# One DRAM replication of 5 MB issued as eight transfers, in a one-core hybrid attention and mLSTM layer

## The chip, the core and the metric

The kernel runs on one core of one Trainium2 chip. Times are device microseconds (us) of that core. The kernel before takes 886.04 us in the median of three runs (885.03 to 887.89). One further execution was recorded with the profiler; all durations below come from it.

## The reference

A decoder layer on 512 tokens of 1024 channels. The input is RMS-normalised and projected once; two branches read the projection, each is gated, projected back, and the two are merged, projected, added to the input and normalised. What matters here is where the position bias comes from.

```
proj = xn @ w_in[layer]
q_a, k_a, v_a, z_a, x_m, z_m, o_m, gates = jnp.split(proj, SPLIT_POINTS, axis=-1)
y_a = dilated_attention(to_heads(q_a), to_heads(k_a), to_heads(v_a), rel_bias)   # 16 heads of 64
y_a = (y_a * jax.nn.silu(z_a)) @ w_pa[layer]
y_m = mlstm_branch(x_m, z_m, o_m, ...) @ w_pb[layer]                             # 4 heads of 512
merged = g_a * y_a + g_m * y_m
h = h + (merged @ w_out[layer]).astype(h.dtype)
# inside the attention, for each head:
bias = rel_bias.astype(jnp.float32)[t5_bucket(jnp.clip(delta, 0, band) * dilation)]
logits = jnp.where(valid, logits + bias, -jnp.inf)
```

The bias depends on the distance between query and key alone, so for one head it is one row of numbers, read at a shifted place for each query.

## The kernel before, in words

**Stages.** Products in f32 precision are made of three fast products each: every operand is split into a high part (`whi`, `xh`, made by ScalarE, ACT) and a low part (`wlo`, `xl`, made by VectorE, DVE), and TensorE (PE) multiplies high by high, high by low and low by high. Weights come in 512 KB chunks (`raw`, 128 rows of 4096 bytes) from DRAM. In order of time PE makes the projection `xm` and the mLSTM scores `S`, then for each of the four mLSTM heads: the output gate `om`, the values `v` (from a copy `xmr` of the projected rows that was stored in DRAM), the numerators `num`, the gate `zm`, the transposes `hT`, and the projection `ym`. Then comes `va`, the values of eight attention heads, and the eight pairs of attention heads (`qa`, `ka`, `za`, `sa`, `pT`, `pv`), the merge gates `gate`, and the projections `ya` and `out`.

**The bias rows.** After the first mLSTM head the function `rel_rows` makes the 16 bias rows of 640 numbers, stores them in DRAM as `fd`, and copies `fd` inside DRAM into `fr`, which holds each row 128 times: 16 x 128 x 640 numbers, 5120 KB, in one transfer. Each attention head later loads its tile `tb` from `fr` with a row step of 639, which gives every partition the row shifted by one.

**What sets the order.** Nothing runs while the kernel is written down: every call is recorded, and a list planner (`Recorder.issue`) replays the recording with estimated durations and writes out one instruction order for each engine. All loads but the last store go through one queue, that of SyncE (SP). A load is placed when its buffer is free in the plan; of the waiting ones the planner looks at about forty in the order of the recording, so a transfer that is recorded late is placed late although nothing holds it. At run time each engine, and SP too, takes its list strictly in order.

**Names and lines.** All instructions carry L333, the line where the recorded calls are made, so the text goes by tiles. `weights` (L423) loads and splits one chunk; `pair_weights` (L573) does it for two chunks that are combined (`s`); `block_v` (L746) loads four `xmr` and makes `v`; `values` (L1019) makes `va` out of four chunks; `rel_rows` is L995.

Of the kernel before, what the change touches and what calls it, by code (L numbers as in the profile page):

```python
# [17 lines left out]
P = 128  # L18
# [6 lines left out]
HEADS_A = 16  # L25
# [312 lines left out]
def hybrid_layer(ctx, tc, a, out):  # L338
    nc = tc.nc
    R = Recorder(nc, a["win"].tensor)  # L340
    V, A, PE, G, SP = (R.engine(e) for e in ("vector", "scalar", "tensor", "gpsimd", "sync"))
# [11 lines left out]
    def slot(name, dt=F32):  # L353
        return tile_of(upool, [P, 516], dt, name, "u", NSLOT)

    def mm_bank(name):
        return tile_of(psum, [P, 512], F32, name, "mm", 2, True)

    def sc_bank(name):
        return tile_of(psum, [P, 512], F32, name, "x", 6, True)  # L360
# [3 lines left out]
    def wide(name, dt=F32):  # L364
        return tile_of(upool, [P, 1280], dt, name, "w1280", NWIDE)

    def wide_t(name, dt=F32R):
        return tile_of(upool, [P, 1408], dt, name, "w1408", NWT)

    def small(name, n):  # L370
        return tile_of(spool, [P, 8], F32, name, "small", NSMALL)[:, :n]

    def const(name, shape, dt=F32):
        return R.buf(lambda: cpool.tile(shape, dt, name=name), shape, dt)

    def raw_chunk(name, p=P):
        return tile_of(wpool, [P, 1024], F32, name, "raw", NRAW)[:p]

    def dram(name, shape):
        return R.buf(lambda: dpool.tile(shape, F32, name=name), shape, F32, dram=True)  # L380
# [42 lines left out]
    def weights(src):  # L423
        R.ahead = AHEAD
        hl = halves(fetch(src))
        R.ahead = 0
        return hl
# [22 lines left out]
    def proj_k(ps, hl, x, k):  # L450
        c = slice(k * P, (k + 1) * P)
        mm3(ps, hl[0][:, c], hl[1][:, c], *x[k], k == 0, k == NK - 1)
# [192 lines left out]
    def proj_t(chunk, name, x=None):  # L645
        hl = weights(a["win"][chunk])
        ps = mm_bank(name)
        for k in range(NK):
            proj_k(ps, hl, x or list(zip(xh, xl)), k)
        return ps  # L650
# [235 lines left out]
    def silu2(ps, name):  # L886
        z = slot(name)[:, :T]
        A.activation(z, ps, AF.Tanh, scale=0.5)
        V.scalar_tensor_tensor(z, z, 1.0, ps, op0=OP.add, op1=OP.mult)
        return z  # L890
# [104 lines left out]
    def rel_rows():  # L995
        onehot = raw_chunk("onehot", 64)[:, :640]
        SP.dma_start(onehot, a["onehot"])
        relb = const("relb", [32, HEADS_A], F32)
        SP.dma_start(relb, a["rel_bias"])
        ohr, rel2 = wide("ohr", F32R)[:64, :640], const("rel2", [64, HEADS_A], F32R)  # L1000
        A.activation(ohr, onehot, AF.Copy)
        A.activation(rel2[:32], relb, AF.Copy)
        V.tensor_sub(rel2[32:], relb, rel2[:32].bitcast(F32))
        lnm = raw_chunk("lnm", 16)[:, :640]
        SP.dma_start(lnm, a["lnmask"])
        frow = raw_chunk("frow", 16)[:, :640]
        for c0 in (0, 320):
            ps = sc_bank("frow")[:16, :320]
            PE.matmul(ps, rel2, ohr[:, c0:c0 + 320], start=True, stop=True)
            V.tensor_add(frow[:, c0:c0 + 320], ps, lnm[:, c0:c0 + 320])  # L1010
        fd = dram("fd", [16, 640])
        SP.dma_start(fd, frow)
        fr = dram("fr", [16, P, 640])
        SP.dma_start(fr, fd[:, None, :].to_broadcast([16, P, 640]))
        return fr

    vals = []

    def values(p):  # L1019
        vv = []  # L1020
        for ps in proj_n(CV + p, "va"):
            for c in range(2):
                v = slot("va", F32R)[:, :512].rearrange("p (h w c) -> p h w c", h=4, w=2)
                src = ps[:, 256 * c:256 * c + 256].rearrange("p (h c) -> p h c", h=4)
                R.ahead = EMPTY
                A.activation(v[:, :, 0, :], src, AF.Copy, scale=0.5)
                V.scalar_tensor_tensor(v[:, :, 1, :], src, 0.5, v[:, :, 0, :].bitcast(F32),
                                       op0=OP.mult, op1=OP.subtract)
                R.ahead = 0
                vv.append(v)  # L1030
        return vv

    wt_of[0] = head_weights(0)
    for h in range(HEADS_M):
        head(h)
        if h == 0:
            fr = rel_rows()


    yaf = []  # L1040
    for p in range(HEADS_A // 2):
        if p % 4 == 0 and p:
            vals.append(values(p))
        vv = vals[-1]
        qps = proj_t(CQ + p, "qa")
        qh = [slot("qh", F32R)[:, :T] for _ in range(2)]
        ql = [slot("ql", F32R)[:, :T] for _ in range(2)]
        for w in range(2):
            o, o2 = 64 * w, 64 - 64 * w
            src = qps[o:o + 64]  # L1050
            A.activation(qh[w][o:o + 64], src, AF.Copy, scale=0.125)
            V.scalar_tensor_tensor(ql[w][o:o + 64], src, 0.125, qh[w][o:o + 64].bitcast(F32),
                                   op0=OP.mult, op1=OP.subtract)
            A.activation(qh[w][o2:o2 + 64], qh[w][o:o + 64].bitcast(F32), AF.Copy)
            A.activation(ql[w][o2:o2 + 64], ql[w][o:o + 64].bitcast(F32), AF.Copy)
        kps = proj_t(CK + p, "ka")
        kk = [slot("kk", F32R)[:, :T] for _ in range(2)]
        for w in range(2):
            src = kps[64 * w:64 * w + 64]
            o, o2 = 64 * w, 64 - 64 * w  # L1060
            A.activation(kk[w][o:o + 64], src, AF.Copy)
            V.tensor_sub(kk[w][o2:o2 + 64], src, kk[w][o:o + 64].bitcast(F32))
        z = silu2(proj_t(CZA + p, "za"), "za")
        ya = slot("ya")[:, :T]
        tmp = slot("yt")[:, :T]
        for w in range(2):
            hd = 2 * p + w
            tb = slot("tb")[:, :512]
            SP.dma_start(tb, fr[hd].then(lambda r: bass.AP(tensor=r.tensor, offset=r.offset + 127,
                                                           ap=[[639, P], [1, 512]])))  # L1070
            pt = wide("p")
            pr = []
            for i in range(NT):
                n = P * (i + 1)
                N = max(n, 256)
                ps = sc_bank("sa")
                qq = slice(i * P, (i + 1) * P)
                PE.matmul(ps[:, :N], qh[w][:, qq], kk[w][:, :N], start=True, stop=False)
                PE.matmul(ps[:, :N], ql[w][:, qq], kk[w][:, :N], start=False, stop=True)
                s = pt[:, P * (i * (i + 1) // 2):][:, :n]  # L1080
                mx, sm = small("mx", 1), small("sm", 1)
                V.tensor_tensor_reduce(s, ps[:, :n], tb[:, 512 - n:], op0=OP.add, op1=OP.min, scale=-1.0,
                                       scalar=3.0e38, accum_out=mx)
                A.activation(s, s, AF.Exp, scale=-1.0, bias=mx, accum_out=sm)
                V.reciprocal(sm, sm)
                V.tensor_scalar(s, s, sm, None, op0=OP.mult)
                pr.append(s)
            po = pv_bank("pv")
            pth, ptl = wide_t("pTh"), wide_t("pTl")
            off = (0, 512, 896, 1152)  # L1090
            for j in range(NT):
                t0 = j * P
                q0 = min(t0, T - 256)
                ps = sc_bank("pT")
                for i in range(j, NT):
                    PE.transpose(ps[:, i * P:(i + 1) * P], pr[i][:, t0:t0 + P], ident)
                th, tl = pth[:, off[j]:off[j] + T - q0], ptl[:, off[j]:off[j] + T - q0]
                if q0 < t0:
                    G.memset(th[:, :t0 - q0].bitcast(F32), 0.0)
                    G.memset(tl[:, :t0 - q0].bitcast(F32), 0.0)  # L1100
                A.activation(th[:, t0 - q0:], ps[:, t0:], AF.Copy)
                V.tensor_sub(tl[:, t0 - q0:], ps[:, t0:], th[:, t0 - q0:].bitcast(F32))
                lv = vv[2 * j + p % 4 // 2][:, 2 * (p % 2) + w].rearrange("p w c -> p (w c)")
                PE.matmul(po[:, q0:], lv, th, start=j == 0, stop=False)
                PE.matmul(po[:, q0:], lv, tl, start=False, stop=j == NT - 1)
            o, o2 = 64 * w, 64 - 64 * w
            A.activation(tmp[o:o + 64], po[o2:o2 + 64], AF.Copy)
            V.tensor_add(ya[o:o + 64], po[o:o + 64], tmp[o:o + 64])
        V.tensor_mul(ya, ya, z)
        yaf.append(ya)  # L1110
# [178 lines left out]
```

## Time and profile before

| what | us |
|---|---|
| median of three runs | 886.04 |
| the profiled execution's own time | 883.73 |
| its span, from the first to the last instruction | 881.8 |
| PE busy | 863.8 (98% of the span) |
| DVE busy | 661.8 (75%) |
| ACT busy | 471.2 (53%) |
| mean share of full clock granted to PE | 0.996 |
| data moved by DMA | 110.00 MB, 125 GB/s in the mean |

The profiled execution took 1.9 us more than its span, for what lies ahead of the first and behind the last instruction. Busy time of PE is modelled, so 98% says that PE has hardly any idle time, not that it is at its peak. The DMA line of the page shows the load on the core's 16 DMA engines: it is heavy in the first 60 us and again around 265 to 290 us, and light elsewhere.

### The profile page before, as it was taken

To read this page: it belongs to the slowest core of one execution; us is meant where nothing else is said; L and a number is where in the kernel's file an instruction comes from. 1 tells how busy PE (TensorE), PEld (TensorE's weight loads), DVE (VectorE), ACT (ScalarE), POOL (GpSimd) and SP (SyncE) were. 2 spreads that over 40 slices of the span, in tenths; PEclk is the share of its full clock that TensorE was granted. 3 is DMA by queue.
4 is the path that set the end of the run, shared out by engine and by line. 5 is a ranking of instruction groups with operands and counts; after the bars stand their busy time and mean duration, and the time that the engine had idled before them with its cause. 6 is when DMAs were issued, how large, how long until landed. Compare 5 with 4: busy or idle time off the path is not lost.

```text
span 881.8 us, 13364 instructions
## 1 busy us (share of the span) xinstructions
PE 863.8 (98%) x4916; PEld 741.7 (84%) x4916; DVE 661.8 (75%) x1361; ACT 471.2 (53%) x879; POOL 10.9 (1%) x70
## 2 busy tenths in 40 slices
PE   7999999999998999999999999999999999999997
PEld 6778877798888889988988888888888899998886
DVE  4899889799557867967865487874778899888533
ACT  7668876655323522551333477654667665674222
POOL 0000000000000000000000000000000000000000
PEclk9999999999999999999999999999999999999999
DMA  9834443234339422511424322212222123356021
GB/s 317 318 132 161 162 166 116 89 123 150 102 121 335 149 72 96 199 61 52 159 81 144 120 82 87 97 60 96 83 77 80 61 73 119 119 170 214 25 72 48
DMA packets 39962, 110.00 MB, mean 125 GB/s; under 512 B 4436, under 2 KB 6228, under 8 KB 39896
## 3 DMA queue, kind: packets, MB, share of 16 engines
q1 hardware_dynamic: 39752, 108.87, 36.0%
q8 instruction: 39, 0.64, 0.3%
q10 hardware_dynamic: 144, 0.26, 0.1%
q14 instruction: 27, 0.22, 0.1%
HBM read 95.97 MB, written 18.39 MB: 130 GB/s over the span
## 4 chain that ended last, share of the span: by engine, by line
PE 89%; DMA 6%; DVE 2%; ACT 1%; SPq 1%; issue 0%; POOL 0%; ACTq 0%
PE ym L333 10%; PE om L333 10%; PE gate L333 9%; PE zm L333 7%; PE xm L333 7%; PE out L333 5%; PE va L333 5%; PE ya L333 5%; PE qa L333 5%; PE za L333 5%; PE ka L333 4%; DMA raw<-in_win_dram 4%; PE S L333 3%; PE num L333 2%; PE sa L333 2%; PE pv L333 2%
## 5 line engine op out<-in xcount | busy, mean ns | idle before, releaser
L333 DVE TENSOR_TENSOR wlo<-raw,whi 128x1024 fp32r<-128x1024 f32 (+1 forms) x126 | 146.9, 1170 | 81.4 <-ACT whi L333 81.0
L333 ACT ACTIVATE whi<-raw 128x1024 fp32r<-128x1024 f32 (+1 forms) x126 | 127.8, 1017 | 145.6 <-PE ym L333 44.8
L333 ACT ACTIVATE whi<-s 128x512 fp32r<-128x512 f32 (+1 forms) x32 | 26.9, 841 | 51.1 <-PE ym L333 11.9
L333 PE MATMUL om<-whi,xh 128*128 128x512 f32 x128 | 51.1, 399 | 0.0
L333 PE MATMUL om<-whi,xl 128*128 128x512 f32 x128 | 50.7, 396 | 0.0
L333 PE MATMUL ym<-yh,whi 128*128 128x512 f32 x128 | 50.7, 396 | 0.0
L333 PE MATMUL om<-wlo,xh 128*128 128x512 f32 x128 | 50.6, 395 | 0.0
L333 PE MATMUL ym<-yl,whi 128*128 128x512 f32 x128 | 50.5, 395 | 0.0
L333 PE MATMUL ym<-yh,wlo 128*128 128x512 f32 x128 | 50.4, 394 | 0.0
L333 ACT ACTIVATE p<-p,mx 128x128 f32<-128x128 f32 (+1 forms) x64 | 35.6, 558 | 14.5 <-DVE mx L333 14.2
L333 DVE CUSTOM_DVE_ANT_0 p<-sa,tb 128x128 f32<-128x128 f32 (+1 forms) x64 | 28.8, 484 | 14.4 <-PE sa L333 14.4
L333 PE MATMUL zm<-th,whi 128*128 128x256 f32 x128 | 36.9, 288 | 0.0
L333 PE MATMUL zm<-tl,whi 128*128 128x256 f32 x128 | 36.5, 285 | 0.0
L333 PE MATMUL zm<-th,wlo 128*128 128x256 f32 x128 | 36.5, 286 | 0.0
L333 PE MATMUL gate<-th,wlo 128*128 128x256 f32 x128 | 36.3, 284 | 0.0
L333 PE MATMUL gate<-tl,whi 128*128 128x256 f32 x128 | 36.1, 282 | 0.0
L333 PE MATMUL gate<-th,whi 128*128 128x256 f32 x128 | 35.9, 282 | 0.0
L333 DVE SCALAR_TENSOR_TENSOR conv<-xm,half,conv 128x512 f32<-128x512 f32 x48 | 35.4, 745 | 0.3
L333 PE MATMUL xm<-xl,whi 128*128 128x512 f32 x88 | 35.3, 401 | 0.0
L333 DVE TENSOR_TENSOR ymacc<-ymacc,ym 128x512 f32<-128x512 f32 x24 | 16.5, 686 | 24.8 <-PE ym L333 24.8
L333 PE MATMUL xm<-xh,wlo 128*128 128x512 f32 x88 | 34.8, 397 | 0.0
L333 PE MATMUL xm<-xh,whi 128*128 128x512 f32 x88 | 34.6, 395 | 0.0
(294 smaller groups left out, 2682.1 us busy)
## 6 DMA issues: line engine op xcount, KB each, us to landing
raw<-in_win_dram SPq DMA_DIRECT2D x94, 512.0 KB, 3.5
raw<-in_wpb_dram SPq DMA_DIRECT2D x16, 512.0 KB, 4.3
fr<-fd SPq DMA_DIRECT2D x1, 5120.0 KB, 21.8
xmd<-xm SPq DMA_DIRECT2D x16, 256.0 KB, 2.2
sxd<-sx SPq DMA_DIRECT2D x16, 256.0 KB, 2.0
xmr<-xmd SPq DMA_DIRECT2D x16, 256.0 KB, 4.8
sxr<-sxd SPq DMA_DIRECT2D x16, 256.0 KB, 4.8
tb<-fr SPq DMA_DIRECT2D x16, 256.0 KB, 3.6
```

The costliest lines, as they stand in the source:

```text
L333: getattr(getattr(self.nc, op.eng), fn)(*a, **k)
```

## The change

`rel_rows` now returns `fd` and an empty `fr`. The copy is made by a new function, `rel_spread(p)`, which copies the two rows of one pair of heads (640 KB). It is called for pair 0 where the whole copy stood, and for pair p + 1 at the head of the attention loop's pass p.

```
-        fr = dram("fr", [16, P, 640])
-        SP.dma_start(fr, fd[:, None, :].to_broadcast([16, P, 640]))
-        return fr
+        return fd, dram("fr", [16, P, 640])
+
+    def rel_spread(p):
+
+        hh = slice(2 * p, 2 * p + 2)
+        SP.dma_start(fr[hh], fd[hh, None, :].to_broadcast([2, P, 640]))
...
         if h == 0:
-            fr = rel_rows()
+            fd, fr = rel_rows()
+            rel_spread(0)
...
+        if p + 1 < HEADS_A // 2:
+            rel_spread(p + 1)
```

The source pattern of the whole copy is 16 rows, each repeated 128 times, of 640 numbers; that of a piece is 2 rows, each repeated 128 times, of 640 numbers.

The planner places the eight pieces on SP's list, the first where the whole copy stood. This is SP's list from the third mLSTM head's gate weights to the fourth head's values (`fr<-fd` a piece, `raw` a weight chunk, `sxr` and `xmr` stored rows that come back):

```order
 L333 DMA raw<-in_win_dram 128x1024
 L333 DMA xmr<-xmd 128x512 x4
-L333 DMA raw<-in_win_dram 128x1024 x4
-L333 DMA sxr<-sxd 128x512 x4
+L333 DMA raw<-in_win_dram 128x1024
+L333 DMA fr<-fd 256x1x640
 L333 DMA raw<-in_win_dram 128x1024 x3
+L333 DMA sxr<-sxd 128x512 x2
+L333 DMA fr<-fd 256x1x640
+L333 DMA sxr<-sxd 128x512 x2
+L333 DMA raw<-in_win_dram 128x1024 x3
+L333 DMA fr<-fd 256x1x640
```

Pieces 2, 3 and 4 now stand between loads that followed each other before. The list goes on, through the fourth head's values and gates to the first weights of `va`:

```order
 L333 DMA raw<-in_wpb_dram 128x1024 x4
 L333 DMA raw<-in_win_dram 128x1024
-L333 DMA xmr<-xmd 128x512 x4
+L333 DMA xmr<-xmd 128x512
+L333 DMA fr<-fd 256x1x640
+L333 DMA xmr<-xmd 128x512 x3
 L333 DMA raw<-in_win_dram 128x1024 x5
+L333 DMA fr<-fd 256x1x640
 L333 DMA sxr<-sxd 128x512 x4
-L333 DMA raw<-in_win_dram 128x1024 x2
+L333 DMA raw<-in_win_dram 128x1024
+L333 DMA fr<-fd 256x1x640
```

Piece 5 stands between the first and the second of the four `xmr` that the fourth head's `v` needs, pieces 6 and 7 ahead of the last chunk of `va`; piece 8 follows a little later, behind four `wpb` chunks. On PE the same products are made; at the fourth head's `v` they stand so:

```order
-L333 MATMUL v<-Bv,xmr 128x128 x8
-L333 MATMUL om<-whi,xh 128x512
-L333 MATMUL v<-Bv,xmr 128x128 x8
-L333 MATMUL om<-wlo,xh 128x512
-L333 MATMUL om<-whi,xl 128x512
-L333 MATMUL om<-whi,xh 128x512
-L333 MATMUL om<-wlo,xh 128x512
-L333 MATMUL om<-whi,xl 128x512
-L333 MATMUL om<-whi,xh 128x512
+L333 MATMUL v<-Bv,xmr 128x128 x4
```

In the new list the four products with the first `xmr` keep their place, seven `om` products follow, and then the twelve products with the other three `xmr`. Further on, in three of the eight pairs of attention heads (the first, second and fifth), some score products, exponentials and splits change places.

## Rows read from the trace of the kernel before

**Rows 1.** First part of the page: busy time and share of the engines
```profile
PE 863.8 (98%) x4916; PEld 741.7 (84%) x4916; DVE 661.8 (75%) x1361; ACT 471.2 (53%) x879; POOL 10.9 (1%) x70
```

**Rows 2.** Waits of PE: us in total, times, longest us
```profile
PE zm L333 <- DVE p L333: 3.5, 1, 3.5
...
PE pv L333 <- ACT pTh L333: 0.5, 1, 0.5
```

**Rows 3.** Chain of waits, 255 to 300 us: start us, us, what
```profile
260.97 22.36 DMA raw<-in_win_dram
...
283.43 1.07 ACT whi L333
...
284.52 1.23 DVE wlo L333
...
286.14 4.62 PE zm L333 x24
290.75 8.12 PE om L333 x35
```

**Rows 4.** Two stretches: us, busy by engine, granted clock, DMA share, GB/s
```profile
265.00:280.00 15.00, 15.00 (x129) 15.00 (x128) 14.13 (x42) 7.19 (x12) 0.00 (x0) 1.00 1.01 331
...
285.00:290.00 5.00, 3.86 (x22) 3.86 (x23) 5.00 (x10) 1.58 (x2) 0.00 (x0) 0.72 0.86 333
```

**Rows 5.** DMA issues, whole run: KB each, median us to landing
```profile
raw<-in_win_dram SPq DMA_DIRECT2D x94, 512.0 KB, 3.5
...
fr<-fd SPq DMA_DIRECT2D x1, 5120.0 KB, 21.8
xmd<-xm SPq DMA_DIRECT2D x16, 256.0 KB, 2.2
...
selr<-in_sel_dram SPq DMA_DIRECT2D x1, 72.0 KB
...
bif<-in_bif_dram SPq DMA_DIRECT2D x1, 0.0 KB
```

**Rows 6.** DMA in 265 to 280 us: GB/s in 40 slices; packets, MB, share
```profile
GB/s 410 389 300 321 375 266 300 362 321 294 328 369 314 280 348 314 294 287 369 300 239 335 341 246 259 298 305 283 287 299 352 355 332 320 407 395 400 412 412 423
...
q1 hardware_dynamic: 1968, 4.95, 100.6%
```

**Rows 7.** SP in order of time, 341 to 436 us: start us, us, what
```profile
342.14 2.48 SPq L333 DMA_DIRECT2D sxr<-sxd  x4
348.05 9.48 SPq L333 DMA_DIRECT2D raw<-in_win_dram  x3
358.40 10.29 SPq L333 DMA_DIRECT2D raw<-in_wpb_dram  x4
...
369.88 1.85 SPq L333 DMA_DIRECT2D xmr<-xmd  x4
...
418.79 0.33 SPq L333 DMA_DIRECT2D raw<-in_win_dram  x1
...
434.63 0.33 SPq L333 DMA_DIRECT2D raw<-in_win_dram  x1
```

**Rows 8.** PE in order of time, at `v` and at `va`
```profile
376.64 1.95 PE L333 MATMUL v<-Bv,xmr 128*128 128x128 f32 x16
378.35 0.48 PE L333 MATMUL om<-whi,xh 128*128 128x512 f32 x1
...
449.69 0.40 PE L333 MATMUL va<-wlo,xh 128*128 128x512 f32 x1
```

**Rows 9.** ACT in order of time, three places
```profile
278.74 0.63 ACT L333 ACTIVATE zm<-c 128x512 f32<-128x512 f32 x1 [2.12 <-DVE c L333]
...
443.81 1.04 ACT L333 ACTIVATE whi<-raw 128x1024 fp32r<-128x1024 f32 x1
...
473.13 1.06 ACT L333 ACTIVATE whi<-raw 128x1024 fp32r<-128x1024 f32 x1 [3.68 <-PE ym L333]
```

**Rows 10.** DVE in order of time, two places
```profile
333.46 0.69 DVE L333 TENSOR_TENSOR s<-raw 128x512 f32<-128x512 f32 x1
...
445.16 1.22 DVE L333 TENSOR_TENSOR wlo<-raw,whi 128x1024 fp32r<-128x1024 f32 x1
```

## The prediction, made before the changed kernel was run

> **What bounds the kernel now.** I read the busy times first: PE is busy for 863.8 of 881.8 us [rows 1]. So the end moves by what PE waits more or less, and by nothing else. The waits of PE come next. One of them belongs to the copy: 3.5 us, once, where `zm` waits for `p` from DVE [rows 2]. The chain of waits around it tells why: a weight chunk issued at 260.97, right behind the copy, lands 22.36 us later, against 3.5 us for such a chunk in the median [rows 3, 5]. Then ACT splits it (1.07), DVE makes the low part (1.23), and PE goes on at 286.14. The copy itself takes 21.8 us to land [rows 5], and the DMA engines are full meanwhile: share 1.01, 331 GB/s [rows 4]. A load issued behind the copy lands just after it; the queue hands over in order.
>
> The stall has a second part. [...] The 24 `zm` products take 4.62 us [rows 3], 0.193 each; in the stretch before PE made 129 products in 15 us, 0.116 each [rows 4]. That is 24 x 0.077 = 1.8 us.
>
> **What goes.** The first piece stands where the copy stood, but is an eighth of it. By the dearest of the prices below it is through 13.1 us after its first packet, about 274.8; the chunk behind it is in at about 276.6. ACT is free for it from 278.74 + 0.63 = 279.4 [rows 9]. So the wait is gone by any price: -3.5 - 1.8 = **-5.3 us**.
>
> **What one piece costs.** The trace has no transfer of this shape, so I bound it. The copy keeps 16 engines full, so each carries a sixteenth of it: 5120/16 = 320 KB (327,680 bytes). Cheap end: a piece is also spread over 16 engines, with 40 KB each. Dear end: a piece has 2 source rows where the copy has 16, and if a transfer is dealt out to the engines by its outermost rows, two engines carry 320 KB each, as much per engine as the copy, while fourteen carry none. The speed of one engine comes from the stretch in which all are full: 4.95 MB in 15 us [rows 6] is 20.6 GB/s for each, and the last six slices, at 395 to 423 GB/s, show 25 to 26. Two engines that have the memory to themselves are nearer to the fast slices, so I take 25 GB/s: 327,680 / 25 = **13.1 us**, with 12.5 (26 GB/s) and 15.9 (20.6 GB/s) as bounds. At the cheap end it is 13.1/8 = 1.6 us.
>
> I take the dear end. [...] Against it speaks only that no row shows it directly.
>
> [...]
>
> **What the dear piece does to the loads behind it.** Every other load has 128 rows and needs all 16 engines, the two loaded ones among them. It lands when those two have worked through what was issued ahead. On one engine a chunk is 32 KB or 1.3 us, an `sxr` or `xmr` 0.65; a landing is seen about 0.5 us later. I keep the clock of the trace before; the 5.3 us shift everything alike.
>
> - Piece 2 starts near 317.5 and ends near 330.6; the two chunks behind it land at 332.4 and 333.7. DVE wants them at 333.46 [rows 10]: nothing.
> - Pieces 3, 4, 5 stand close together. The second `sxr` of 342.14 [rows 7] is through at about 345.4 (an unhindered store of that size takes 2.2 to land [rows 5]), and piece 3 starts. From there the two engines are never free until the second `xmr` is in: piece 3, two `sxr` (1.3), three chunks (3.9), piece 4, four `wpb` chunks and one more (6.5), the first `xmr` (0.65), piece 5, the second `xmr` (0.65). That is 3 x 13.1 + 13.0 = 52.3, so 397.7, seen at 398.2. In the trace these loads were issued by 370.8 [rows 7], so the queue, not the issue, sets the landing.
> - PE wants the first `xmr` at 376.64 [rows 8]. In the new order eight passes of `v` follow (16 take 1.71 to the next `om` [rows 8], so 0.85), then seven `om` at 8.12/35 = 0.232 [rows 3], 1.6 in all: the second `xmr` is wanted at 379.1. PE stands first for the first `xmr`, then for the second, and goes on at 398.2: **+19.1 us**. What is behind it on PE is all the rest of `om`; nothing else can run.
> - Piece 6 is issued behind the chunk of 418.79 [rows 7]: the two engines have that chunk until 421.4, piece 6 until 434.5, four `sxr` until 437.1, a chunk until 438.4, piece 7 until 451.5, and the last chunk of `va`, issued at 434.63 [rows 7], until 452.8: in at 453.3. ACT wants it at 443.81 [rows 9]; then ACT's 1.07 and DVE's 1.23 [rows 3] end at 455.7. In the trace that low part began at 445.16 on DVE [rows 10] and PE used it at 449.69 [rows 8]: **+6.0 us**. DVE and ACT stand too, but PE has 22 us of `va` left for them to catch up.
> - Piece 8 ends near 471; the chunk behind it is in by 472.7 and wanted at 473.13 [rows 9], by then 8 us later: nothing.
> - Each of the two stalls is longer than the 3.5 us after which the clock was halved. I count the same 1.8 for each, **+3.6**; the bounds are 0 and, for four restarts, 7.
>
> **The changed places in the attention.** In three pairs the fourth score product moves ahead on PE and its reduction ahead of a split on DVE. PE waits 0.5 us in all for `pTh` there now [rows 2]; I add 0.1 for each pair, **+0.3**, bounds 0 and 1.5. Eight issues for one on SP cost about 0.6 us of SP each, which is idle for most of the run.
>
> **Sum.** -5.3 + 19.1 + 6.0 + 3.6 + 0.3 = +23.7 us. On the profiled execution 883.73 becomes 907.4; on the median, which lies 2.3 higher, 886.04 becomes **909.7**. A piece counts three times in the first stall and twice in the second, so its bounds move the sum by 5 x (-0.6 to +2.8) = -3 to +14; the clock moves it by -3.6 to +3.4. The likeliest case's own range is 900 to 924.
>
> **Rivals.**
> 1. *A piece is spread over 16 engines (faster).* Then it holds up what is behind it by 1.6 us. The `xmr` after it land by about 378.5, before PE wants them (379.1), the last chunk of `va` by 440, and all that remains is the stall that goes: -5.3 + 0.3 = -5.0, or 881.0. It decides if an engine holds a piece for under about 3 us. For it: the copy did use 16 engines. Against it: the two rows.
> 2. *Two engines, but they don't hold the others up fully*, because loads overtake or pieces are issued sooner than I think, so that one of the three pieces in the row falls into a gap: 13.1 less, 896.6. Against it: in the trace nothing issued behind the copy landed ahead of it.
> 3. *Worse*: engines at 15.9 us a piece and halved clock after each restart, 909.7 + 14 + 3.4 = 927.
> 4. *The change does nothing that shows*: the stall at 283 stays because another load or DVE is as late, and the pieces find room: 886. Against it: ACT is free at 279.4 and the chunk is early by any price.
>
> **Chances.** Forecast 0.80, rival 1 0.08, rival 2 0.06, rival 3 0.03, rival 4 0.03. From the forecast's own range and rival 2 nearly all of 8 in 10 comes, so the range is 893 to 924; rivals 1 and 4 stay outside. A change of 0.3% (2.7 us) is about what a measurement of this kernel can tell. Faster by more than that: rival 1, 0.08. Within it: rival 4, 0.04 with the edges of others. Slower: 0.88.
>
> **What would show it.** Right: in the list of DMA issues eight `fr<-fd` with a landing of some 14 to 30 us, the length of the old copy although each is an eighth; a DMA share near 2/16 while one runs; two new waits of PE, `v` for `xmr` (some 19 us in two parts) and `va` for ACT or DVE (about 6); no wait of `zm` for `p` and a granted clock of 1.0 near 285, but a lower one after the two new stalls. Wrong: pieces that land in 3 to 5 us. Then the forecast falls at the price of a piece, and rival 1 is what happened. If the pieces are as long as I say and PE still doesn't wait at `v`, the step on the order of the queue is wrong.

## The result, and the profile of the changed kernel

The changed kernel takes 910.39 us in the median (907.63 to 912.12) against 886.18 for the kernel before; the ratio is 1.027, with a 95% interval of 1.0247 to 1.0294. The forecast was 909.7 us. Its profiled execution took 907.63 us, with a span of 905.8, against 883.73 and 881.8.

PE's busy time grew by 7.5 us with the same 4916 instructions, so some of them ran slower (first part of the page, as [rows 1]):

```profile
PE 871.3 (96%) x4916; PEld 745.8 (82%) x4916; DVE 662.1 (73%) x1361; ACT 471.2 (52%) x879; POOL 10.0 (1%) x70
```

The waits of PE (us in total, times, longest) are to be read beside [rows 2]:

```profile
PE v L333 <- DMA xmr<-xmd: 16.5, 4, 8.3
PE xm L333 <- ACT whi L333: 5.3, 2, 5.0
PE va L333 <- ACT whi L333: 4.3, 1, 4.3
...
PE va L333 <- DVE wlo L333: 0.5, 1, 0.5
```

The wait of `zm` for `p` is gone; two others have come, at `v` and at `va`. The wait at `xm` is the one at the start of the program and was 5.1 before. The list of DMA issues (count, KB each, median us to landing) stands beside [rows 5]:

```profile
raw<-in_win_dram SPq DMA_DIRECT2D x94, 512.0 KB, 3.4
...
fr<-fd SPq DMA_DIRECT2D x8, 640.0 KB
...
sxr<-sxd SPq DMA_DIRECT2D x16, 256.0 KB, 11.1
```

No landing is found for any `fr<-fd`, as for `selr` and `bif` before. By itself that doesn't tell how many engines carry a transfer: in the kernel before the list finds none for `lnm` either, which has 16 rows as `fd` has, and in the changed kernel it loses nine that it had, among them that of `go`, which fills 128 rows (a row of the list before, then one of the list now):

```profile
lnm<-in_lnmask_dram SPq DMA_DIRECT2D x1, 40.0 KB
```

```profile
go<-in_norm_out_g_dram SPq DMA_DIRECT2D x1, 512.0 KB
```

What a piece does is seen from the load behind it. The same list, cut to what was issued between 260 and 261 us, has the chunk that SP issued at 260.46, right after piece 1:

```profile
fr<-fd SPq DMA_DIRECT2D x1, 640.0 KB
raw<-in_win_dram SPq DMA_DIRECT2D x1, 512.0 KB, 16.2
```

It lands at 276.6, where the median chunk takes 3.4. The stretches (busy by engine, granted clock, DMA share, GB/s) answer to [rows 4]:

```profile
285.00:290.00 5.00, 5.00 (x25) 4.07 (x24) 4.76 (x8) 3.25 (x6) 0.00 (x0) 1.00 0.54 157
380.00:385.00 5.00, 4.33 (x15) 3.32 (x13) 3.42 (x9) 2.35 (x7) 0.13 (x2) 0.60 0.37 133
385.00:390.00 5.00, 0.00 (x0) 0.00 (x0) 1.01 (x4) 0.00 (x0) 0.00 (x0) 0.74 0.29 108
470.00:475.00 5.00, 4.54 (x10) 3.25 (x11) 5.00 (x8) 1.31 (x3) 0.00 (x0) 0.50 0.13 52
```

In the last one piece 8 is alone with the memory: a share of 0.13 of 16 engines is 2.1 engines, and they move 52 GB/s, 26 for each. That is the width and the speed of the dear end. The same row has a granted clock of 0.50, after the stall at `va`; between 285 and 290 it is 1.00 now, where it was 0.72 (from 288 to 290 it was 0.50).

The chain of waits shows both stalls (start us, us, what), first the stretch that held the old one:

```profile
282.20 3.03 PE zm L333 x24
285.24 8.12 PE om L333 x35
...
295.17 2.68 PE v L333 x24
```

The 24 `zm` that took 4.62 us in [rows 3] take 3.03. Then the stretch from 340 to 480 us:

```profile
365.47 27.13 DMA xmr<-xmd x2
392.60 0.04 issue
392.64 5.31 PE v L333 x24
397.95 12.33 PE om L333 x53
...
450.69 18.06 DMA raw<-in_win_dram
...
468.83 1.06 ACT whi L333
...
469.92 1.24 DVE wlo L333
...
471.19 9.02 PE va L333 x28
```

Two `xmr` one after the other, 27.13 us, hold PE; then a chunk of 18.06 us holds ACT, DVE and PE. The 24 `v` after the stall take 5.31 us, where the 24 of the head before take 2.68.

**The difference by steps.** PE has the same instructions in both traces, nearly all in the same order. I took the start of the same product in both and subtracted; where the difference changes, time is gained or lost. Each line is one profiled execution against the profiled execution before; "ahead" is the difference at 279 us, before the first piece can matter:

```
kernel                 ahead   zm    291-370   v      va    at the end
changed                -0.4   -5.1   +0.5    +21.0   +7.8   +24.0
e1_repeats_first       +3.1   -5.1    0.0      0.0    0.0    -1.6
e2_narrow_345          +3.5   -5.1    0.0    +21.5    0.0   +20.2
e3_narrow_67           +1.0   -5.1    0.0      0.0   +8.3    +4.6
e4_four_rows           +3.6   -5.1   +1.4    +11.7   +4.9   +16.7
f1_piece5_behind_xmr   +2.5   -5.1   +0.5    +10.7   +8.3   +17.0
f2_pieces_on_act_queue +1.5   -5.1   +5.5    +13.1    0.0   +15.3
f3_narrow_128          +4.9   -5.1   +0.8      0.0    0.0    +0.8
f4_one_copy_later      +1.0   -5.1   +1.0      0.0    0.0    -3.2
g1_act_queue_45_behind +0.9   -5.1   +4.6     +2.5    0.0    +4.4
```

What is left over from the columns lies in the attention, up to 1.1 us. The "ahead" column is no effect of any edit: up to there all kernels do the same, and the differences arise in the first 40 us and at the second head's `v` near 210 us. It moves single executions by up to 5 us, so an edit worth 5 is read from its own step, and from medians of several runs.

### The profile page after: what moved, and what is told of

The parts are those of the page before. It is cut to its first block, busy times and chain, and to the rows that moved or that the text cites. A ratio compares the mean times of both kernels' runs of the same rounds, so it can differ in the third digit from the quotient of the medians.

```text
span 905.8 us, 13376 instructions
## 1 busy us (share of the span) xinstructions
PE 871.3 (96%) x4916; PEld 745.8 (82%) x4916; DVE 662.1 (73%) x1361; ACT 471.2 (52%) x879; POOL 10.0 (1%) x70
## 4 chain that ended last, share of the span: by engine, by line
PE 87%; DMA 7%; DVE 3%; ACT 1%; issue 1%; SPq 0%; POOL 0%; DVEq 0%; ACTq 0%
PE xm L333 10%; PE gate L333 9%; PE ym L333 8%; PE om L333 8%; PE zm L333 6%; PE out L333 5%; PE qa L333 5%; PE ya L333 5%; PE za L333 5%; PE va L333 5%; PE ka L333 4%; DMA raw<-in_win_dram 4%; DMA xmr<-xmd 4%; PE S L333 3%; PE num L333 3%; PE sa L333 2%
## 5 line engine op out<-in xcount | busy, mean ns | idle before, releaser
L333 ACT ACTIVATE whi<-s 128x512 fp32r<-128x512 f32 (+1 forms) x32 | 26.9, 842 | 51.2 <-PE zm L333 13.1
L333 PE MATMUL v<-Bv,xmr 128*128 128x128 f32 x128 | 19.3, 314 | 16.5 <-DMA xmr<-xmd 16.5
```

The lines of the kernel that those rows point to most:

```text
L333: getattr(getattr(self.nc, op.eng), fn)(*a, **k)
```

## The experiments

In all of them theory A is the prediction's: a piece of two outermost rows is carried by two engines, and a load issued behind it in the same queue lands when those two have worked through it.

**e1_repeats_first: the width alone.** Places, bytes and order are those of the changed kernel.

```
-        SP.dma_start(fr[hh], fd[hh, None, :].to_broadcast([2, P, 640]))
+        SP.dma_start(fr[hh].rearrange("h p f -> p h f"),
+                     fd[None, hh, :].to_broadcast([P, 2, 640]))
```

> All eight pieces keep their places and their bytes; only the pattern of each is turned: 128 repeats outermost, the two rows inside, instead of two rows outermost. Theory A (a piece of two outermost rows is carried by two engines, and they hold up the loads behind it): spread over 16 engines a piece holds the queue for some 1.6 us, the waits of v for xmr (16.5 us) and of va for whi and wlo (4.8) go, the granted clock stays 1.0; span 881.8 - 5.3 + 0.3 = 876.8, time about 881, 5 below the kernel before. Theory B (the places and the number of the transfers, or their bytes late in the run, cost whatever carries them): as the changed kernel, span about 906, time about 910. Theory C (the changed order of PE in v and in the attention pairs costs): the same order stands here, so a good part of the 24 us stays, span over 885.

Measured: 882.44 us against 887.55, ratio 0.9933 (0.9913 to 0.9952). The DMA issues between 263.5 and 264.5 us, which hold the first piece and the chunk behind it:

```profile
fr<-fd SPq DMA_DIRECT2D x1, 640.0 KB, 6.5
raw<-in_win_dram SPq DMA_DIRECT2D x1, 512.0 KB, 7.1
```

The piece has a landing now, and the chunk takes 7.1 us for 16.2. Of PE's waits at `v` and `va` in this kernel one row is left, and this wait is at the second head's `v`, before the first piece:

```profile
PE v L333 <- DMA xmr<-xmd: 1.6, 1, 1.6
```

The step table has -5.1 and nothing else. Theories B (places, number, bytes) and C (order of PE) fall: with the same places and the same order the loss of 29 us is gone. The pattern of a piece made the change slower, not the splitting.

**e2_narrow_345 and e3_narrow_67: the two stalls apart.** The pattern of e1, but with two rows outermost for pieces 3 to 5, or for 6 and 7:

```
+        if p in (2, 3, 4):      # e3: (5, 6)
+            SP.dma_start(fr[hh], fd[hh, None, :].to_broadcast([2, P, 640]))
+        else: ...               # as in e1
```

> Pieces 3, 4 and 5 keep two rows outermost, the other five have the repeats outermost. Theory A with the terms of the prediction: the wait of v for xmr stays at about 16.5 us in two parts, with some 5 us of halved clock around it, the wait of va goes: span 876.8 + 16.5 + 5 = 898, time about 902. Theory B: 906 and 910. If the second stall were only a consequence of the first (loads late once, late again), it would stay too: span about 905.

> Pieces 6 and 7 alone keep two rows outermost. Theory A: no wait of v for xmr; va waits about 4.8 us for whi and wlo with 2.6 us of halved clock behind it; span 876.8 + 7.4 = 884, time about 888. If the stall at va came from the loads that the stall at v delayed, nothing would be left here: span 877, time 881. Theory B: 906 and 910.

Measured: e2 903.24 us, ratio 1.0171 (1.0148 to 1.0194); e3 890.11 us, 1.0027 (1.001 to 1.0045). The waits of PE in e2, then in e3:

```profile
PE v L333 <- DMA xmr<-xmd: 18.0, 3, 8.1
```

```profile
PE va L333 <- ACT whi L333: 5.1, 1, 5.1
...
PE va L333 <- DVE wlo L333: 0.5, 1, 0.5
```

Of the 18.0 us, 1.9 are at the second head, before the first piece; 16.1 are at the fourth. Each stall comes with its own pieces and without the other: +21.5 at `v`, +8.3 at `va`, and in the changed kernel +21.0 and +7.8. They add up.

**f3_narrow_128: the three pieces that the prediction called free.** As e2, with pieces 1, 2 and 8 narrow.

> Pieces 1, 2 and 8 keep two rows outermost, the other five have the repeats outermost. The prediction gave these three no cost: what stands behind them is wanted later. Theory A: no wait of zm, none of v over 2 us, none of va; span 880 as with all eight turned (876 to 882), time 882. Theory B (each narrow piece costs its share of the 29 us): 3/8 of it, 11 us more, span 891, time 893.

Measured: 882.31 us, ratio 0.9939 (0.9916 to 0.9962), as with all eight turned. Of 0.8 us between 291 and 370, 0.6 come at `v` of the third head, where PE waits 0.4 for `xmr`; `va` has no wait.

**e4_four_rows: does the time go with the bytes or with the rows?** Four transfers of twice the size, in the old pattern:

```
+        R.swap[R.ops[-1]] = [] if p % 2 else [("dma_start",
+            (fr[2*p:2*p+4], fd[2*p:2*p+4, None, :].to_broadcast([4, P, 640])), {})]
```

> Four transfers of four rows each (1280 KB) stand where pieces 1, 3, 5 and 7 stood; the places of 2, 4, 6 and 8 are empty; the pattern is that of the changed kernel (rows outermost). Theory A: four engines carry 320 KB each, so a transfer of twice the bytes holds the queue as long as a piece did, about 13 us; the chunk behind the first one lands 16 us after its issue as before (16.17). Two fewer in the row at v make the second xmr 13.1 us earlier, so the first stall goes and the second is about 379.5 - 374.2 = 5.3 us with 2.6 of halved clock; at va one transfer instead of two, no stall; span 876.8 + 8 = 885, time 889. If the time went with the bytes of a transfer, each would hold 26 us, the chunk behind the first would land 29 us after its issue, and the span would stay near 906.

Measured: 900.07 us, ratio 1.0134 (1.0109 to 1.0159). What the engines moved after the first transfer, in 40 slices, first for the changed kernel (259.5 to 266 us), then for e4 (263.5 to 270.7):

```profile
GB/s 353 429 302 277 76 126 101 126 101 101 50 0 0 32 16 47 63 32 63 63 32 32 16 63 47 47 63 47 47 63 47 47 63 47 47 47 47 63 47 47
```

```profile
GB/s 228 296 341 296 273 250 182 91 68 114 37 0 14 43 28 43 57 85 100 100 100 85 100 100 71 85 85 114 114 114 71 85 114 114 114 100 85 100 114 114
```

Some 50 GB/s with two rows and some 100 with four: the width follows the rows. The chunk behind the transfer has no landing in the list. The first `sxr` behind it lands 18.4 us after the transfer's issue (263.83 to 282.22); if 1280 KB had taken 26 us it would be 31. So a transfer of twice the bytes holds the queue as long as a piece. The span, 898.3, is 13 above what I expected by theory A. By the step table 3.6 of that were there ahead of the first transfer, 1.4 came between 291 and 370 us, 3.8 at `v` (11.7 for 7.9) and 4.9 at `va` (where I had nothing). For `v` the reason is in SP's own order of issue in e4 (start us, us, what):

```profile
369.85 0.43 SPq L334 DMA_DIRECT2D xmr<-xmd  x1
370.33 0.61 SPq L334 DMA_DIRECT2D fr<-fd  x1
370.99 9.11 SPq L334 DMA_DIRECT2D xmr<-xmd  x3
```

With fewer transfers in the row the engines are free before 369.85 (from 368.3 to 369.2 us they move nothing), and the third transfer starts when it is issued, not 13.1 us earlier: the second `xmr` lands at 388.4 (370.33 + 18.1), not at 379.5, and PE waits 9.2 us at the fourth head's `v`. The same at `va`: the last transfer was issued at 445.20 and the chunk behind it landed at 462.13. I had taken away 13.1 us for each missing piece; a queue that runs dry gives back less.

**f1_piece5_behind_xmr: the order in the queue.** One transfer moved, nothing else:

```
+        if p == 4:
+            R.late.append((R.ops[-1], xmr_last[3]))   # issued behind that xmr
```

> The changed kernel with one transfer moved: piece 5 is issued behind all four xmr of the fourth head, not between the first and the second; every other instruction keeps its place. Theory A (a load waits for the two engines to work through what was issued ahead of it in its queue): all four xmr land together, about where the first landed (379.4); PE stands once at v for 7.7 us, with some 2.5 of halved clock, where the two stalls took 21.0 in all; the stall at va stays (8.4). Span about 10.5 below the changed kernel, 895, time near 900, 1.5% over the kernel before. Theory D (the pieces take bandwidth from the loads wherever they stand, order does not matter): the second xmr is late as before, span 906, time 910.

Measured: 900.06 us, ratio 1.0135 (1.0106 to 1.0165). PE in order of time at `v`:

```profile
382.73 2.05 PE L338 MATMUL v<-Bv,xmr 128*128 128x128 f32 x8 [8.00 <-DMA xmr<-xmd]
...
387.56 3.00 PE L338 MATMUL v<-Bv,xmr 128*128 128x128 f32 x24
```

One stall of 8.00 us, and the other 24 `v` follow without a wait. The step at `v` is +10.7, which is 10.3 below the changed kernel's, for an expected 10.5 below. Theory D falls; the place of a piece in the queue is worth 10 us.

**f2_pieces_on_act_queue and g1_act_queue_45_behind: another queue.** The pieces keep two rows outermost, but ACT issues them; in g1 pieces 4 and 5 go behind the four `xmr` besides.

```
-                getattr(getattr(self.nc, op.eng), fn)(*a, **k)
+                eng = "scalar" if op in self.other else op.eng    # the eight pieces
+                getattr(getattr(self.nc, eng), fn)(*a, **k)
```

> The eight pieces keep their two-row pattern and their places, but are issued by ACT into its own queue; the loads stay on SP's. Theory A says it is the order within one queue that holds the loads up: now a load shares the two engines with a piece, its part on them takes at most twice as long (a chunk 2.6 for 1.3 us, an xmr 1.3 for 0.65), so no wait over 1 us of v for xmr and none of va beyond 1; span as with the repeats outermost, 877 to 884, time 880 to 886; ACT may stand a few us where the first piece waits for the row fd. Theory E (the two engines work a transfer through before they take the next, whatever queue it came from): the loads are as late as in the changed kernel, v waits some 16 us, span 900 to 908, time 905 to 912.

Measured: 900.97 us, ratio 1.0146 (1.0116 to 1.0175), which is neither what A nor what E gave. The chunk behind piece 1 landed 6.2 us after its issue, where it took 16.2, and `va` had no wait: on another queue than the piece's this load did not stand behind it. But `v` waited. A row of PE's waits (10.9 of it at the fourth head), and one of SP's from 371.7 to 400 us:

```profile
PE v L334 <- DMA xmr<-xmd: 13.9, 5, 9.7
```

```profile
SPq L334 <- DMA fr<-fd: 14.8, 1, 14.8
```

SP didn't issue the second `xmr` until it had waited 14.8 us for piece 4. In the list this `xmr` is the eighth transfer behind piece 4. Two other traces have such a wait at the same distance: the changed kernel 5.6 us for piece 4, at the second `xmr` too, and the kernel before 3.9 us for the whole copy, at the `wpb` chunk of 282.15, which is the eighth transfer behind it (the copy landed at 260.31 + 21.8 = 282.1). A row of SP's waits in the kernel before, and one of SP in order of time:

```profile
SPq L333 <- DMA fr<-fd: 3.9, 1, 3.9
```

```profile
282.15 8.94 SPq L333 DMA_DIRECT2D raw<-in_wpb_dram  x4
```

What makes it the eighth, no run shows. In g1 the transfer eight ahead of the second `xmr` is a weight chunk:

> As with the pieces on ACT's queue, but pieces 4 and 5 are issued behind the four xmr of the fourth head. [...] Theory E (a load on SP's queue waits behind a piece on the shared engines): v still waits 8 us or more, span over 890, time over 893.

Measured: 888.98 us, ratio 1.0032 (1.0008 to 1.0056). The waits of PE:

```profile
PE ym L339 <- DVE ymacc L339: 2.3, 1, 2.3
PE om L339 <- ACT tho L339: 2.2, 1, 2.2
...
PE v L339 <- DMA xmr<-xmd: 0.8, 2, 0.4
```

Theory E falls: `v` waits 0.8 us, and none of it at the fourth head. From 369 to 400 us SP waits for no piece; in f2 its wait of 14.8 us had made `xmr` late. The time is still 0.3% above the kernel before, for costs that I had not counted: +4.6 between 291 and 370 us and +2.5 at `v` in the step table. For the second, ACT in order of time:

```profile
374.32 5.90 ACTq L339 DMA_DIRECT2D fr<-fd  x2
380.26 0.62 ACT L339 ACTIVATE E<-Abc,aT 128x384 f32<-128x384 f32 x1 [5.32 <-issue]
```

Two narrow pieces behind each other keep ACT 5.90 us at issuing them, its `tho` are late, and `om` waits. The first holds the wait of `ym`, 2.3 us in f2 too. It follows the chunk behind piece 2, which landed 6.5 us after its issue; in the changed kernel that chunk was issued ahead of the piece and landed after 3.4. That it shares engines with the piece is argued, not tried, and the rest of the 4.6 is open.

**f4_one_copy_later: the kernel before with its one copy moved.** It is issued behind the third head's `xmr`, into a stretch without loads; the pattern is the old one.

```
         SP.dma_start(fr, fd[:, None, :].to_broadcast([16, P, 640]))
+        R.late.append((R.ops[-1], lambda: xmr_last[2]))
```

> The kernel before with its one copy of 16 rows moved: issued behind the four xmr of the third head (about 294 us), into some 18 us in which SP issues nothing; all else in place. If the 3.5 us wait of zm and its halved clock came only from the chunk queued behind the copy, they go: span 880, time 882 like the eight turned pieces. If the copy then holds up the chunks issued at 313 to 317, wanted from 317 on (ACT and DVE wait, PE stands as long): up to 4 us come back, span 880 to 884, time 882 to 887.

Measured: 880.15 us against 888.12, ratio 0.9909 (0.9884 to 0.9933): faster than both kernels. The DMA issues between 291 and 300 us:

```profile
fr<-fd SPq DMA_DIRECT2D x1, 5120.0 KB, 22.0
```

The copy is as long as ever and nothing stands behind it until 310.70. It gives the same step of -5.1 and then +1.0, of which 0.7 is a wait of `ym`. Between f4 and e1 the medians differ by 2.3 us, the steps by 0.5 the other way, and the ratios' intervals overlap: these runs don't tell them apart.

## Why the prediction was right, step by step

- **What goes, -5.3: measured -5.1.** The wait is gone by 3.6 and the clock by 1.5 (24 `zm` in 3.03 for 4.62). It goes in every kernel here, narrow pieces or broad, on either queue: the chunk behind a piece is early by any price, as the prediction put it.
- **The price of a piece, 13.1 us on two engines: right.** The chunk behind piece 1 was forecast at about 276.6 and landed at 276.6. To the tenth that is luck: the changed kernel issued it 0.5 us earlier than the trace before, so from its issue it took 16.2 us for a forecast of 15.6. That two engines carry a piece was my estimate from its two rows, and no row of the trace before shows it; the 2.1 engines of piece 8 do. A chunk that is alone has a share of 0.84 of the 16 engines (trace before, 476.4 to 478.3 us). The bounds of 12.5 and 15.9 were not needed: the two engines made 26 GB/s each, the upper end of what I had read. e1 excludes the cheap end for this pattern and shows what rival 1 would have been: its forecast of -5.0 is what e1 measured (882.44 - 887.55 = -5.1).
- **The row of pieces at `v`, +19.1 and 1.8 for the clock: measured +21.0.** The second `xmr` was forecast at 398.2 in the time of the trace before, which is 393.2 here (5.0 earlier by the step table); PE went on at 392.64. The make-up is a little different. PE waited 7.70 and 8.31 us, 16.0 in all. Between the two stalls, 8 `v` and 7 `om` took 4.84 us for the 2.45 of the forecast, at a lower clock, but the second stall was waiting for a fixed time, so these 2.4 us came out of it. Behind it the clock cost 5.31 - 2.68 = 2.6, where I had 1.8.
- **The row at `va`, +6.0 and 1.8: measured +7.8.** The waits were 4.3 + 0.5, the rest of the step, 3.0, is clock. The wait is 1.2 less than forecast and the clock 1.2 more; the sum is right partly by luck.
- **Pieces 1, 2 and 8 free: right**, by f3 (0.0 at `v` and `va`), and +0.5 between 291 and 370 us that the forecast lacked; its cause is open.
- **The attention, +0.3: measured about +0.1.** Eight issues on SP cost nothing that shows.
- The steps make +24.4, with -0.4 ahead of them +24.0, for a forecast of +23.7. Rivals 2 and 3 would have shown at `v` as +8 or as some +30.

One premise of the row at `v` was wrong without changing its sum: that the loads are issued by 370.8, as in the trace before. In the changed kernel SP stands for piece 4 before it issues the second `xmr`, the wait that f2 has too (a row of SP's waits from 365 to 375 us, then SP from 372 to 384 us in order of time):

```profile
SPq L333 <- DMA fr<-fd: 5.6, 1, 5.6
```

```profile
372.47 11.58 SPq L333 DMA_DIRECT2D xmr<-xmd  x3
```

Piece 5, issued at 366.25, still held that `xmr` up longer than its late issue did. f1 tells the two apart: there SP stands 4.9 us for piece 4 too, before the third `xmr`, but with piece 5 behind the loads there is no second stall.

What the experiments correct is the reason behind "the two engines are never free". It held for the changed kernel, since three pieces in a row keep the queue full; where the queue runs dry (e4) a piece counts from its issue. And the queue's order was only one way in which a slow transfer holds up others; f2 showed a second (14.8 us at the eighth transfer behind a piece), and g1 a third (ACT took 5.90 us to issue two pieces).

## What to carry to other kernels

Before splitting a transfer, look at what its outermost count becomes: the split took a copy from 16 engines to 2 per piece (shares of 1.01 and 0.13), and an engine then had as many bytes to move for one piece as for the whole copy. Write the broadcast with the 128 repeats outermost, or leave the copy whole and issue it where no load follows for its length; both gained here what the split was able to gain (ratios of 0.9933 and 0.9909). The price of a slow transfer here isn't its own landing, whose data no engine waited for, but that of the loads issued behind it, so read it from them.

## What was not expected of the hardware

- Issuing takes long behind a slow transfer. In e4 SP spent 9.11 us on three `xmr` behind a narrow transfer, in the changed kernel 11.58, in g1 ACT 5.90 us on two pieces; one issue alone is mostly 0.3 to 0.7 us. Why, no run shows. For ACT, which computes, it was a stall of 5.32 us.
- A spread piece of 640 KB landed 6.5 us after its issue though it held the loads behind it up by far less: in e1 one `xmr` landed at 373.00, the piece behind it at 374.61 and the next `xmr` at 375.28.
- The two new stalls, of 16.0 and 4.8 us, cost 2.6 and 3.0 us in granted clock behind them, where the stall of 3.5 us before cost 1.5.
